# Products with the values in an attention kernel: summing their two parts before the transposes instead of after

## The chip, the cores and the metric

One core of one Trainium2 chip. The metric is the device time of one execution in microseconds; the table below gives the median of three runs.

## The reference

One layer over 2048 tokens of width 1024, in float32: `h = RMSNorm(x) @ w_in`, four groups of four attention heads of width 64 on the columns of `h`, and an output projection with a residual. Cut to what the change touches:

```python
# A: dilated attention, (window, rate) in (128,1), (512,4), (2048,16), merged by softmax denominators
# B: sliding window of 128 with sinks      C: differential attention, two softmax maps
# D: compressed / selected / sliding-window branches, gated
p = exp(scores + bias - max)            # 128 queries by their keys, per head
o = (p @ v) / den                       # every group and branch ends in such a product
y = concat(o_A, o_B, o_C, o_D) * silu(gate)
x = x + y @ w_out
```

## The kernel before

All matrix products run in a float32 form whose operands are split into a high and a low part (`xh`/`xl`, `ph`/`pl`), because one pass over the high part alone would lose digits. The values lie in SBUF as tiles of 128 keys by 128 columns: 64 columns high part, 64 columns low part. A product with the values (`prods`, L407 to L423) uses such a tile as the stationary operand and moves the transposed probabilities past it, once `ph`, once `pl`. So one PSUM tile `o` of 128 partitions collects, for up to four tiles of 128 queries side by side, the transposed output twice: partitions 0 to 63 hold the products with the high part of the values, partitions 64 to 127 those with the low part. Their sum is the output.

A *unit* is such a tile's worth of work: two query tiles of one head in groups C (32 units) and in the selected branch of D (32), four query tiles or heads in the sliding-window branch of D (16), its compressed branch (16), group A (48, the last 16 of them for rate 1, "A1") and group B (16): 160 units, 64 of two tiles and 96 of four. There is one PSUM bank for `o` (pool `ps_o`, bufs=1), so the first product of the next unit waits until the bank is free. At the end of a unit, inside `drive` (L368 to L373), ScalarE copies the bank to the SBUF tile `ot`, and that copy alone frees the bank. Later the unit's `close` calls `o_turn` (L429 to L449): TensorE transposes `ot` in blocks of 128 columns (L434), and the two halves of each transposed block are added on the way out of PSUM, either by one VectorE reduction (L438) or by a ScalarE copy (L441) and a VectorE addition (L443). Where the unit has row weights (`wt`: one over the denominator, times a gate), GpSimd multiplies by them afterwards (L447).

The order of the work is made when the program is written out: `drive` keeps a planned time per engine (`T`), a planned time at which each PSUM bank comes free (`take`, `give`) and a list of steps that wait for a planned time (`defer`). It issues whichever step is planned ready first: transposing a finished unit's `ot`, products, transposing probabilities (`turn_bank`, L392 to L402), scores. When none is ready it issues *filler*: projections of later groups (L832), and later the output projection (L2147). The output projection runs over the token tiles twice, first with the groups C and D (384 matmuls, available when the selected branch has stored a tile), then with A and B (available when A1 and B have stored one). Every engine then runs its instructions in the written order.

On DMA queues nothing is issued by the lines that change.

Of the kernel before, what the change touches and what calls it, by code (L numbers as in the profile page):

```python
# [102 lines left out]
def tile_hybrid_heads(ctx, tc, a):  # L103
# [34 lines left out]
    TILT = -100.0  # L138
# [80 lines left out]
    def give(slot, t):  # L219
        ring[slot[0]][slot[1]] = t  # L220
# [93 lines left out]
    def drive(units, nbuf=3, depth=2, eager=lambda left: False):  # L314

        us, steps = [], []
        tq, pq, cq = [], [], []
        tdone = []

# [7 lines left out]

        while len(us) < len(units) or steps or tq or pq or cq:
            poll()
# [33 lines left out]
            elif c[1] == 1:  # L363
# [3 lines left out]
                if bi == len(u["banks"]) - 1:  # L367
                    u.get("after", lambda: None)()  # L368
                    ot = u["pool"].tile([128, u["n"] * 128], F32, name="ot", bufs=1)
                    A.activation(ot, u["po"][:, :u["n"] * 128], AF.Copy)  # L370
                    e = op("ACT", av(u["n"] * 128), T["PE"] + 120.0)
                    give(u["slot"], e)
                    cq.append((k, e, ot))  # L373
            elif c[1] == 2:
# [6 lines left out]
            elif c[1] == 3:  # L381
                steps.pop(0)[1]()
            else:
                fill_step()

    def turn_bank(u, bi):
# [42 lines left out]
    def o_turn(ot, n, dst, wt=None):  # L429

        slot = take("pt")
        ps = ps_t.tile([128, 512], F32, name="pt")
        for i in range(n):
            PE.transpose(ps[:, i * 128:(i + 1) * 128], ot[:, i * 128:(i + 1) * 128], ident)  # L434
        e = op("PE", 109.0 * n) + 60.0
        p3 = ps[:, :n * 128].rearrange("p (t c) -> p t c", c=128)
        if max(T["DVE"], max(T["ACT"], e) + av(n * 64) + 120.0) + vv(n * 64) > max(T["DVE"], e) + vv(n * 128) + TILT:
            V.tensor_reduce(dst, p3.rearrange("p t (i d) -> p t d i", i=2), AX.X, OP.add)  # L438
            e = op("DVE", vv(n * 128), e)
        else:  # L440
            A.activation(dst, p3[:, :, 0:64], AF.Copy)  # L441
            e = op("ACT", av(n * 64), e)
            V.tensor_tensor(dst, dst, p3[:, :, 64:128], op=OP.add)  # L443
            e = op("DVE", vv(n * 64), e)
        give(slot, e)
        if wt is not None:
            G.tensor_tensor(dst, dst, wt.unsqueeze(2).broadcast_to([128, n, 64]), op=OP.mult)  # L447
            e = op("POOL", 147.0 + 1.67 * n * 64, e)
        return e  # L449
# [1776 lines left out]
```

## Time and profile before

| | |
|---|---|
| median of three runs (lowest, highest) | 1803.11 us (1802.24, 1807.85) |
| the profiled execution: its time, its span | 1810.59 us, 1808.8 us |
| busy: TensorE (PE), VectorE (DVE), ScalarE (ACT), GpSimd (POOL) | 95%, 74%, 59%, 38% of the span |
| chain that ended last | PE 72%, DVE 11%, DMA 6% |

PE rows are matmuls and transposes, PEld rows weight loads beside them. A matmul's row lasts longer than the time to the next one's start, since they are pipelined; the price of one in a series is the distance between starts. `x4` in a time line means four in a row; the number in brackets is idle time of the engine and what ended it.

### The profile page before, as it was taken

How to read it: one execution, taken by the hardware profiler on the slowest of the kernel's cores; microseconds unless marked ns; L12 is line 12 of the kernel's file. 1: busy time of each engine (PE TensorE's matmuls, PEld its weight loads, DVE VectorE, ACT ScalarE, POOL GpSimd, SP SyncE). 2: the span in 40 equal slices, each digit the busy share in tenths (PEclk: the TensorE clock that was granted, in tenths of full speed). 3: DMA queues.
4: the chain of work that ended last, by engine and by line, in shares of the span. 5: the costliest groups of instructions: out<-in, count | busy, mean ns of one | idle time of the engine just before them, and what ended most of it. 6: DMA issues, size and time to landing. Idle time of an engine off the chain costs nothing.

```text
span 1808.8 us, 31757 instructions
## 1 busy us (share of the span) xinstructions
PE 1720.8 (95%) x10035; PEld 1515.1 (84%) x10035; DVE 1335.6 (74%) x4072; ACT 1067.6 (59%) x2582; POOL 695.0 (38%) x841
## 2 busy tenths in 40 slices
PE   7999999899989999799999999999989999989998
PEld 6878878788778888688888789999979999779876
DVE  5446788888898888388855858888576777878873
ACT  4445556665575665366745647676566666567661
POOL 4667653545454455311245552322311111422331
PEclk9999999999999999899999999999999999999999
DMA  7763655235353533653276542332276878889975
GB/s 241 227 205 115 184 161 173 80 105 178 104 164 91 188 98 116 188 153 90 68 215 201 160 134 58 109 100 81 83 232 196 245 241 277 244 267 280 327 247 187
DMA packets 283480, 308.24 MB, mean 170 GB/s; under 512 B 80256, under 2 KB 201216, under 8 KB 282640
## 3 DMA queue, kind: packets, MB, share of 16 engines
q1 hardware_dynamic: 283312, 306.21, 55.1%
q8 instruction: 80, 1.31, 0.3%
q14 instruction: 88, 0.72, 0.1%
HBM read 219.47 MB, written 86.92 MB: 169 GB/s over the span
## 4 chain that ended last, share of the span: by engine, by line
PE 72%; DVE 11%; DMA 6%; issue 3%; ACT 2%; SPq 2%; POOL 2%; DVEq 0%; ACTq 0%; POOLq 0%
PE j L832 27%; PE o L421 11%; PE pt L392 9%; PE j L2147 9%; PE s L942 6%; PE s L1638 4%; PE pt L434 3%; SPq L156 2%; PE s L1328 2%; DVE pl L402 2%; DVE wb L621 1%; DMA wb<-tkA 1%; DVE pa L944 1%; PE pt L740 1%; DMA tc<-sq 1%
## 5 line engine op out<-in xcount | busy, mean ns | idle before, releaser
L832 PE MATMUL j<-wb,xh 128*128 128x512 f32 (+2 forms) x2048 | 622.9, 385 | 20.1 <-ACT wb L617 8.4
L832 PEld LDWEIGHTS j<-wb,xh 128*128 128x128 f32 x2048 | 374.3, 192 | 69.3 <-DVE wb L621 13.0
L832 PE MATMUL j<-wb,xl 128*128 128x512 f32 (+2 forms) x1024 | 386.8, 378 | 0.6 <-POOL xl L576 0.6
L398 ACT ACTIVATE ph<-pt 128x512 fp32r<-128x512 f32 (+4 forms) x486 | 264.2, 575 | 155.0 <-PE pt L392 140.6
L402 DVE TENSOR_TENSOR pl<-pt,ph 128x512 fp32r<-128x512 f32 (+4 forms) x486 | 311.6, 659 | 38.9 <-ACT ph L398 37.8
L832 PEld LDWEIGHTS j<-wb,xl 128*128 128x128 f32 x1024 | 195.3, 191 | 26.3 <-POOL xl L576 1.5
L678 POOL TENSOR_TENSOR ss<-ss,expo 128x6 f32<-128x6 f32 (+2 forms) x64 | 116.2, 1816 | 227.2 <-DVE ss L676 172.6
L576 POOL TENSOR_TENSOR xl<-xt,xh 128x512 fp32r<-128x512 f32 x112 | 151.8, 1355 | 9.3
L370 ACT ACTIVATE ot<-o 128x512 f32<-128x512 f32 (+1 forms) x160 | 81.4, 509 | 109.4 <-PE o L421 108.6
L2101 POOL TENSOR_TENSOR xt<-xt,sq 128x512 f32<-128x512 f32 x32 | 41.1, 1286 | 232.1 <-DVE sq L2099 167.6
L942 PE MATMUL s<-keys,Q 128*128 128x512 f32 (+3 forms) x320 | 112.7, 397 | 7.9 <-DVE mx L944 4.6
L570 POOL TENSOR_SCALAR xh<-xt 128x512 fp32r<-128x512 f32 x128 | 83.3, 651 | 91.8 <-DMA xt<-in_xt_dram 49.4
L944 DVE CUSTOM_DVE_ANT_0 prow<-s,Hs 128x512 f32<-128x512 f32 (+3 forms) x160 | 94.7, 606 | 19.2 <-PE s L942 18.4
L944 DVE CUSTOM_DVE_ANT_0 pa<-s,H 128x512 f32<-128x512 f32 (+3 forms) x160 | 93.8, 604 | 17.1 <-PE s L942 16.6
L1058 DVE SCALAR_TENSOR_TENSOR pa<-pb,ra,pa 128x1024 f32<-128x1024 f32 (+4 forms) x96 | 101.9, 1089 | 2.3
L944 DVE CUSTOM_DVE_ANT_0 pb<-s,H 128x512 f32<-128x512 f32 (+3 forms) x160 | 93.3, 604 | 9.9 <-PE s L942 9.7
L1654 ACT ACTIVATE ap<-ap,AO 128x128 f32<-128x128 f32 (+1 forms) x192 | 86.4, 456 | 13.4 <-DVE AO L1648 13.1
L673 DVE TENSOR_REDUCE ss<-sq 128x6 f32<-128x384 f32 (+2 forms) x64 | 39.4, 615 | 72.2 <-ACT sq L663 71.4
L659 ACT ACTIVATE stqk<-j 128x512 f32<-128x512 f32 x64 | 38.2, 597 | 90.5 <-PE j L832 90.5
L434 PE MATMUL pt<-ident,ot 128*128 128x128 f32 x512 | 85.2, 279 | 5.5 <-DVE pl L402 3.2
L1042 ACT ACTIVATE pa<-pa,nm 128x128 f32<-128x128 f32 (+7 forms) x64 | 76.9, 1202 | 18.7 <-DVE nm L950 18.5
L1042 ACT ACTIVATE pb<-pb,nm 128x128 f32<-128x128 f32 (+7 forms) x64 | 76.8, 1201 | 14.2 <-DVE nm L950 14.1
(266 smaller groups left out, 4222.6 us busy)
## 6 DMA issues: line engine op xcount, KB each, us to landing
xt<-in_xt_dram SPq DMA_DIRECT2D x128, 256.0 KB, 3.5
xr<-in_x_dram SPq DMA_DIRECT2D x16, 512.0 KB, 5.6
Q<-tqC SPq DMA_DIRECT2D x64, 128.0 KB, 3.4
DQ<-tqD SPq DMA_DIRECT2D x16, 512.0 KB, 4.9
raw<-gate_d SPq DMA_DIRECT2D x32, 256.0 KB, 4.7
stqk<-in_x_dram SPq DMA_DIRECT2D x32, 256.0 KB, 4.6
acc_d<-stqk SPq DMA_DIRECT2D x32, 256.0 KB, 3.6
stqk<-acc_d SPq DMA_DIRECT2D x32, 256.0 KB, 4.3
```

Source lines behind the costliest of these rows:

```text
L392: PE.transpose(ps[:rows, x * 128:(x + 1) * 128], src(), ident)
L398: A.activation(ph[:rows, :n], ps[:rows, :n], AF.Copy)
L402: V.tensor_tensor(pl[:rows, :n], ps[:rows, :n], ph[:rows, :n], op=OP.subtract)
L421: PE.matmul(u["po"][:, c0:c0 + wd], lhsT=lhsT(), rhs=x[:rows, col:col + wd], start=u["k"] == 1, stop=u["k"] == total, skip_group_check=True)
L434: PE.transpose(ps[:, i * 128:(i + 1) * 128], ot[:, i * 128:(i + 1) * 128], ident)
L576: G.tensor_tensor(l, xt, h, op=OP.subtract)
L678: G.tensor_tensor(ss[:, :nh], ss[:, :nh], expo[:, :nh], op=OP.pow)
L832: PE.matmul(ps[:, :n], lhsT=xx[:, ks], rhs=W[k][ww][:, lo:hi], start=(k == 0 and i == 0), stop=(k == KT - 1 and i == 2))
L942: PE.matmul(ps[:, :n], lhsT=q(), rhs=k[:, k0:k0 + n], start=(i == 0), stop=(i == np_ - 1))
L944: V.tensor_tensor_reduce(st["row"][:, k0:k0 + n], ps[:, :n], rev(H, t * 128 + 127 - k0, n), 1.0, LOW, OP.add, OP.max, st["mx"][:, ci:ci + 1])
L1042: A.activation(row[:, :nk], row[:, :nk], AF.Exp, bias=nm, accum_out=den[:, i, m:m + 1])
L2147: PE.matmul(ps, lhsT=xx[:, ks], rhs=OW[half, (k, c)][ww], start=(x == 0 and k == 0 and i == 0), stop=(x == len(halves) - 1 and k == 3 and ...
```

## The change

`o_turn` no longer adds halves. Right behind a unit's last product, `half_sums` forms the sum in the transposed layout: ScalarE copies the low part of the first half of the columns to partitions 0 to 63 of `ot` and the high part of the second half to partitions 64 to 127; VectorE adds the other part from PSUM onto each. `ot` is now half as wide, with the first half of the query tiles in the upper 64 partitions and the second half in the lower, and has two buffers instead of one. The bank `o` is free after the second addition. `o_turn` transposes half as many blocks and reads them once, on VectorE together with the row weights, or on ScalarE with the GpSimd multiplication behind it; a planned comparison picks. The planner counts the new steps.

```diff
-                    ot = u["pool"].tile([128, u["n"] * 128], F32, name="ot", bufs=1)
-                    A.activation(ot, u["po"][:, :u["n"] * 128], AF.Copy)
-                    e = op("ACT", av(u["n"] * 128), T["PE"] + 120.0)
-                    give(u["slot"], e)
-                    cq.append((k, e, ot))
+                    summing.append(k)
+                    half_sums(u, lambda ot, e, k=k: turned(k, ot, e))
...
+    def half_sums(u, then):
+        po, m = u["po"], u["n"] * 64
+        ot = u["pool"].tile([128, m], F32, name="ot", bufs=2)
+        A.activation(ot[0:64], po[64:128, 0:m], AF.Copy)
+        e1 = op("ACT", av(m), T["PE"] + 120.0)
+        A.activation(ot[64:128], po[0:64, m:2 * m], AF.Copy)
+        e2 = op("ACT", av(m), T["PE"] + 120.0)
+
+        def add():
+            V.tensor_tensor(ot[0:64], po[0:64, 0:m], ot[0:64], op=OP.add)
+            op("DVE", vv(m), e1)
+            V.tensor_tensor(ot[64:128], po[64:128, m:2 * m], ot[64:128], op=OP.add)
+            e = op("DVE", vv(m), e2)
+            give(u["slot"], e)
+            then(ot, e)
+        defer(e1, add)
...
-        for i in range(n):
+        k = n // 2
+        for i in range(k):
             PE.transpose(ps[:, i * 128:(i + 1) * 128], ot[:, i * 128:(i + 1) * 128], ident)
...
-            V.tensor_reduce(dst, p3.rearrange("p t (i d) -> p t d i", i=2), AX.X, OP.add)
-            e = op("DVE", vv(n * 128), e)
+        on_dve = max(T["DVE"], e) + vv(n * 64) < max(T["ACT"], e) + av(n * 64) + (0.0 if wt is None else 600.0)
+        if on_dve:
+            if wt is None:
+                V.tensor_copy(dst, src)
+            else:
+                V.tensor_tensor(dst, src, w4, op=OP.mult)
...
+            A.activation(dst, src, AF.Copy)
             e = op("ACT", av(n * 64), e)
-            V.tensor_tensor(dst, dst, p3[:, :, 64:128], op=OP.add)
...
+            if wt is not None:
+                G.tensor_tensor(dst, dst, w4, op=OP.mult)
```

Over the whole program the written order has 512 transposes of `ot` before and 256 now; on ScalarE 160 copies out of `o` before and 320 of half the width now; on VectorE no addition onto `ot` before and 320 now. Which operation empties the transposed block changes too: 86 VectorE reductions and 74 ScalarE copies, each with a VectorE addition, before; 63 VectorE multiplications, 6 VectorE copies and 91 ScalarE copies now. The GpSimd multiplications by row weights go from 112 to 49.

Three places of the written order, before and with the change (line numbers of the change are its own: L434 became L455, L421 L441, L392 L412, L832 L859, L942 L969, L2147 L2174).

ScalarE at a unit's end late in the program, before:

```order
L1957 ACTIVATE ap,bden<-ap,bnm 128x256 x2
L370 ACTIVATE ot<-o 128x512
L398 ACTIVATE ph<-pt 128x512
L1957 ACTIVATE ap,bden<-ap,bnm 128x256 x2
L441 ACTIVATE AO<-pt 128x4x64
```

and with the change:

```order
L2142 ACTIVATE xh<-pt 128x512
L392 ACTIVATE ot<-o 64x256
L394 ACTIVATE ot<-o 64x256
L418 ACTIVATE ph<-pt 128x512
L1681 ACTIVATE ap,AO<-ap,AO 128x256 x4
L470 ACTIVATE AO<-pt 128x4x64
```

One copy became two of half the width, and the first VectorE addition waits for a count that only the second copy raises.

TensorE around the last projection matmul (`j<-wb`), in the selected branch of group D (`Qs`, `Qb` are its queries, `prow` probabilities, `VSs` values), before:

```order
L832 MATMUL j<-wb,xh 128x416 x2
L832 MATMUL j<-wb,xl 128x416
L740 MATMUL pt<-ident,stqk 128x128 x8
L942 MATMUL s<-keys,Qs 128x512
L942 MATMUL s<-keys,Qb 128x512
```

and with the change:

```order
L859 MATMUL j<-wb,xh 128x416 x2
L859 MATMUL j<-wb,xl 128x416
L441 MATMUL o<-ph,VSs 128x256
L441 MATMUL o<-pl,VSs 128x256
L441 MATMUL o<-ph,VSs 128x256
L441 MATMUL o<-pl,VSs 128x256
L412 MATMUL pt<-ident,prow_13249 128x128
```

The last projection moved forward. From it to the next filler, the first output matmul, 119 matmuls stand before and 338 with the change (132 products with `VSs`, 121 transposes of probabilities, 66 score matmuls in 33 chunks, 19 other transposes). By the first score of this branch 2730 projection matmuls have been written before, 2832 now.

TensorE behind the last output matmul of groups C and D, in the stage of A1 (`s<-wb` scores, `o<-..,wb` products) and B (`BK,BQ` scores, `BV` products), before:

```order
L2147 MATMUL j<-wb,xl 128x512
L1638 MATMUL s<-wb 128x256 x4
L392 MATMUL pt<-ident,ap 128x128 x4
L1638 MATMUL s<-wb 128x256 x4
L421 MATMUL o<-ph,wb 128x256
```

and a piece of the same stage with the change:

```order
L441 MATMUL o<-ph,BV 128x256
L441 MATMUL o<-pl,BV 128x256
L455 MATMUL pt<-ident,ot 128x128 x2
L1665 MATMUL s<-wb 128x128 x2
L1665 MATMUL s<-wb 128x256 x6
L1967 MATMUL s<-BK,BQ 128x256 x8
L412 MATMUL pt<-ident,ap 128x128 x7
```

Here 112 matmuls stand between the last output matmul of C and D and the first of A and B before, and 254 with the change (78 products, 80 score matmuls, 70 transposes of probabilities, 18 of `ot`, 8 others), and a unit's `ot` is transposed right behind its last product. By the first score of B, 219 output matmuls have been written before, 330 now.

## Rows read from the trace of the kernel before

**Rows 1.** The page: busy time of each engine, instructions.

```profile
PE 1720.8 (95%) x10035; PEld 1515.1 (84%) x10035; DVE 1335.6 (74%) x4072; ACT 1067.6 (59%) x2582; POOL 695.0 (38%) x841
```

**Rows 2.** The page: the chain that ended last, by engine.

```profile
PE 72%; DVE 11%; DMA 6%; issue 3%; ACT 2%; SPq 2%; POOL 2%; DVEq 0%; ACTq 0%; POOLq 0%
```

**Rows 3.** Time line of PE: start, length, engine, line, count; series of transposes and their successors.

```profile
1289.67 0.38 PE L434 MATMUL pt<-ident,ot 128*128 128x128 f32 x2
1289.81 0.36 PE L421 MATMUL o<-ph,VSs 128*128 128x256 f32 x1
...
1315.93 0.60 PE L740 MATMUL pt<-ident,stqk 128*128 128x128 f32 x4
1316.29 0.48 PE L942 MATMUL s<-keys,Qs 128*128 128x512 f32 x1
```

**Rows 4.** Groups by form: busy us, mean ns | idle before.

```profile
L370 ACT ACTIVATE ot<-o 128x512 f32<-128x512 f32 x96 | 57.0, 594 | 68.8 <-PE o L421 68.1 <-ACT xh L2115 0.2
L370 ACT ACTIVATE ot<-o 128x256 f32<-128x256 f32 x64 | 24.4, 381 | 40.6 <-PE o L421 40.5
...
L441 ACT ACTIVATE O<-pt 128x128 f32<-128x128 f32 x14 | 3.9, 278 | 7.4 <-PE pt L434 5.0 <-DMA yC<-O 2.4
...
L402 DVE TENSOR_TENSOR pl<-pt,ph 64x512 fp32r<-64x512 f32 x4 | 2.6, 670 | 0.0
...
L438 DVE TENSOR_REDUCE AO<-pt 128x256 f32<-128x512 f32 x30 | 20.7, 690 | 19.3 <-PE pt L434 19.0
L438 DVE TENSOR_REDUCE Os<-pt 128x128 f32<-128x256 f32 x21 | 8.9, 425 | 13.5 <-PE pt L434 12.9 <-POOL Os L1545 0.6
...
L443 DVE TENSOR_TENSOR AO<-AO,pt 128x256 f32<-128x256 f32 x18 | 7.5, 415 | 1.8 <-ACT AO L441 1.7
...
L443 DVE TENSOR_TENSOR O<-O,pt 128x128 f32<-128x128 f32 x14 | 3.8, 268 | 2.1 <-ACT O L441 2.1
```

**Rows 5.** Time line of all engines: from a unit's last product to its transposes.

```profile
1611.02 0.28 PE L421 MATMUL o<-pl,wb 128*128 128x128 f32 x1
...
1611.33 0.60 ACT L370 ACTIVATE ot<-o 128x512 f32<-128x512 f32 x1
...
1611.98 0.66 PE L434 MATMUL pt<-ident,ot 128*128 128x128 f32 x4 [0.23 <-ACT ot L370]
```

**Rows 6.** Windows: length, busy us (instructions) by engine, granted clock; A, then the stretches without filler.

```profile
1365.00:1527.00 162.00, 161.80 (x984) 151.99 (x983) 114.74 (x435) 104.10 (x356) 27.84 (x19) 1.00 0.79 246
...
1310.50:1339.90 29.40, 24.75 (x122) 17.65 (x120) 23.80 (x65) 19.68 (x32) 2.66 (x3) 0.88 0.81 271
1606.00:1630.60 24.60, 18.40 (x114) 16.17 (x113) 16.73 (x62) 14.62 (x45) 8.59 (x14) 0.79 0.76 226
```

**Rows 7.** Time line: VectorE in the second stretch.

```profile
1607.04 0.41 DVE L1643 CUSTOM_DVE_ANT_0 ap<-s,wb 128x256 f32<-128x256 f32 x1
...
1607.38 0.42 DVE L1643 CUSTOM_DVE_ANT_0 ap<-s,wb 128x256 f32<-128x256 f32 x1
...
1617.60 1.28 DVE L402 TENSOR_TENSOR pl<-pt,ph 128x512 fp32r<-128x512 f32 x2
```

**Rows 8.** Time line of PE: products at full and at the lower clock.

```profile
1290.01 0.28 PE L421 MATMUL o<-pl,VSs 128*128 128x256 f32 x1
1290.13 0.28 PE L421 MATMUL o<-ph,VSs 128*128 128x256 f32 x1
...
1620.80 0.42 PE L421 MATMUL o<-ph,BV 128*128 128x256 f32 x1
1621.01 0.41 PE L421 MATMUL o<-pl,BV 128*128 128x256 f32 x1
```

**Rows 9.** Waits of PE: us in total, times, longest.

```profile
PE o L421 <- DVE pl L402: 13.4, 17, 2.3
...
PE s L942 <- DVE mx L944: 8.0, 13, 2.6
...
PE pt L434 <- ACT ot L370: 1.5, 4, 0.6
```

More of the change, by code (lines that the diff above doesn't have):

```diff
@@ L317, in drive @@
         tq, pq, cq = [], [], []
-        tdone = []
+        tdone, summing = [], []
         def new_unit():
@@ L326, in new_unit, with turned @@
                 tq.append((len(us) - 1, bi))
-        while len(us) < len(units) or steps or tq or pq or cq:
+        def turned(k, ot, e):
+            summing.remove(k)
+            cq.append((k, e, ot))
+        while len(us) < len(units) or steps or tq or pq or cq or summing:
             poll()
@@ L432, in o_turn @@
         ps = ps_t.tile([128, 512], F32, name="pt")
-        for i in range(n):
+        k = n // 2
+        for i in range(k):
             PE.transpose(ps[:, i * 128:(i + 1) * 128], ot[:, i * 128:(i + 1) * 128], ident)
-        e = op("PE", 109.0 * n) + 60.0
-        p3 = ps[:, :n * 128].rearrange("p (t c) -> p t c", c=128)
-        if max(T["DVE"], max(T["ACT"], e) + av(n * 64) + 120.0) + vv(n * 64) > max(T["DVE"], e) + vv(n * 128) + TILT:
-            V.tensor_reduce(dst, p3.rearrange("p t (i d) -> p t d i", i=2), AX.X, OP.add)
-            e = op("DVE", vv(n * 128), e)
+        e = op("PE", 109.0 * k) + 60.0
+        src = ps[:, :n * 64].rearrange("p (i h d) -> p h i d", h=2, d=64)
+        dst = dst.rearrange("p (h i) d -> p h i d", h=2)
+        if wt is not None:
+            w4 = wt.rearrange("p (h i) -> p h i", h=2).unsqueeze(3).broadcast_to([128, 2, k, 64])
+        on_dve = max(T["DVE"], e) + vv(n * 64) < max(T["ACT"], e) + av(n * 64) + (0.0 if wt is None else 600.0)
[4 more added lines that the diff above has]
+                V.tensor_tensor(dst, src, w4, op=OP.mult)
+            e = op("DVE", vv(n * 64), e)
+            give(slot, e)
         else:
-            A.activation(dst, p3[:, :, 0:64], AF.Copy)
+            A.activation(dst, src, AF.Copy)
             e = op("ACT", av(n * 64), e)
-            V.tensor_tensor(dst, dst, p3[:, :, 64:128], op=OP.add)
[L444 to L448, printed above, removed]
+            give(slot, e)
+            if wt is not None:
+                G.tensor_tensor(dst, dst, w4, op=OP.mult)
+                e = op("POOL", 147.0 + 1.67 * n * 64, e)
         return e
```

## The prediction

> **What bounds the kernel now.** I read the page first: TensorE is busy for 95% of the span, VectorE 74%, ScalarE 59% [rows 1]. The chain of waits that ended last says the same: 72% of it is TensorE, 11% VectorE, 6% transfers [rows 2]. So an instruction taken off TensorE is worth about its step, wherever TensorE has something else ready. The windows show where it has: in group A's first stage TensorE is busy for 161.8 of 162 us and VectorE for 114.7 [rows 6]. They also show two stretches where it has not: from the last projection to the first output matmul (1310.5 to 1339.9) and from the last output matmul of C and D to the first of A and B (1606.0 to 1630.6). There the planner has no filler, VectorE is busy for 23.8 of 29.4 and 16.7 of 24.6 us, and the granted clock averages 0.88 and 0.79. A product that follows the next after 0.12 us elsewhere takes 0.21 us there, the 1.2 instead of the 2.4 GHz level [rows 8]. What happens to these stretches decides how much of a TensorE saving is kept.
>
> **The sum goes against the profiled execution** (1810.59 us; 7.5 us, 0.4%, above the median 1803.11). The difference found is then taken off the median. Repeated measurements of this kernel cannot tell less than about 0.3%, 5.4 us, from no change.
>
> **Transposes removed, 256.** A series of two has its successor 0.14 us after its start, one of four 0.36 us [rows 3]: two more cost 0.22, so 0.11 us each. 256 x 0.11 = **28.2 us less** on TensorE. For the same transposes the Trainium skill, "TensorE: Matmul & The Clock Gate", section "Wait — 56ns, not 53.3ns?", gives 55.6 ns from start to start for 128 columns at full clock. By it the removal would be worth 256 x 0.0556 = 14.2 us. The rows of these float32 transposes say twice that, and I take the rows.
>
> **ScalarE.** 96 copies of 594 ns and 64 of 381 ns go (81.4 us) [rows 4]. 320 half-wide ones come: 192 of 256 columns at the 381 ns of that width, 128 of 128 columns at the 278 ns of that width, 109 us. The transposed block leaves through ScalarE 91 times instead of 74, some 5 us. In all +33 us on an engine busy for 59% of the span: hidden, except for the order in which it delivers (below).
>
> **VectorE.** 320 additions come. Half the partitions cost the same as all: a subtraction over 64 partitions took 670 ns, as long as over 128 (1.28 us for two in a row, 0.64 each) [rows 4, 7]. So 192 x 0.415 + 128 x 0.268 = 114 us. 86 reductions go (47 of 0.69, 39 of 0.42: 49 us) and 74 additions (49 of 0.415, 25 of 0.27: 27 us). 69 multiplications or copies come (39 of 0.415, 30 of 0.27: 24 us). Net **+62 us**, 74% of the span becoming some 78%. GpSimd, busy for 38%, loses 63 multiplications.
>
> Where TensorE is full this is covered, but not all of it. TensorE waited 13.4 us for the low halves of the transposed probabilities and 8.0 us for score maxima, both from VectorE [rows 9]. VectorE's busy time grows by 5%; if such waits grow by no more, that is 1 us, if VectorE's lag doubles them in its fullest stages, 10 us. I take **+4 us**, nearer the low end since the planner counts the new passes and writes the followers later.
>
> **The bank `o` and the transposes come later.** Before, the copy starts 0.31 us after the last product's start and lasts 0.60, and the transposes follow 0.96 us after that start [rows 5]. Now the first addition waits for both copies: 0.31 + 0.28 + 0.38, then two additions of 0.41, about 1.8 us. So **0.8 us more per unit**, both for the transposes and for the next unit's first product, which needs the only bank. Counting what the written order puts behind a unit's last product (0.11 us a transpose, 0.12 us per 256 columns), 21 of 160 units now have less than the wait needs (3 before), short by 12 us in all, 10 of it in 13 units of A1 and B. Most of these lie in the second stretch and are counted there; for the others **+2.5 us**.
>
> **The filler moves forward.** To bridge the longer wait the planner spends filler sooner: 102 more projection matmuls before the selected branch, 111 more output matmuls before group B. These are no extra work, but the two stretches without filler grow.
>
> First stretch: from 119 matmuls to 338. TensorE's own steps: 140 transposes at 0.11, 132 products at 0.12, 66 score matmuls of 13 us: 44 us (18 us before). VectorE: 33 score chunks at 0.64 for 512 columns and 0.34 for 256, 18 us; 30 subtractions at 0.64, 19; 14 half additions, 4; closes and the gates of two output tiles, 7: 48 us. The stretch before is mostly scores, each waiting for a bank that VectorE empties; the new one is mixed, and both engines are nearly level. At least it takes 48 us, at VectorE's share of before (23.8 of 29.4) 59. TensorE then loses 4 to 15 us against 11 before: -7 to +4, taken as **+1 us**.
>
> Second stretch: from 112 matmuls to 254, whose own steps are 28.5 us (12.7 before). VectorE's 16.7 us per 112 matmuls [rows 6] make 38 us, with half additions in place of the old ones 42. The pace of before, 24.6 us per 112, would make 56. That pace contains a wait for a load that a longer stretch need not repeat, but the new one has nine closes with 0.8 us more each, several with transposes right behind the last product. I take 48. TensorE loses 19.5 us there against 11.9: **+7.6 us** (bounds +2 and +16).
>
> **Sum:** -28.2 + 4 + 2.5 + 1 + 7.6 = **-13 us**, so 1797.5 us on the profiled execution's scale and **1790 us** against the median, 0.7% less. Chance 0.43.
>
> **Rivals.**
>
> *The whole saving arrives.* The stretches are VectorE's in both kernels, and the loads that held up the second one get time. Then only 2 us are lost: 1777 us. For it: the first stretch is level on both engines. Against: the half additions land exactly where VectorE leads. Chance 0.18.
>
> *The stretches eat it.* The second runs at the pace of before (+16), the first gains 4, VectorE's lag costs 8: 28 us, no change, 1803 us. For it: the clock fell in both stretches before, and fewer TensorE steps beside VectorE's keep it low longer. Chance 0.21.
>
> *Slower: TensorE waits for the bank.* One bank, and now two engines in turn must empty it. The first product of the next unit stands in TensorE's order at a planned time; behind it stand filler and scores that could run. If VectorE reaches the additions late, everything behind stands. The order covers 139 units, so the lag of VectorE decides: from 13 / 139 = 0.09 us per unit nothing is left of the gain, from 0.13 us it is slower by over 0.3%. A single subtraction of 0.64 us ahead of every third addition is 0.2 us, 28 us, hence 1818 us. For it: VectorE already makes products wait in 17 places, up to 2.3 us [rows 9]. Against: the copy that freed the bank until now made the transposes wait 1.5 us in all. Chance 0.16.
>
> *The transposes are cheap.* If a transpose is worth its 0.05 us between others, the removal brings 14 us and the losses above take them: 1802 us, no change. This is where the rule of the page named above leads; the trace speaks against it, with 0.22 us for two. Chance 0.02.
>
> That the change does not do what it says has no room: the written order has 256 transposes instead of 512.
>
> **Numbers.** Faster by over 0.3% (under 1797.7): 0.43 + 0.18 = 0.61. Within: 0.21 + 0.02 = 0.23. Slower: 0.16. The range runs from 1773 us (the whole saving, with a stretch shortened) to 1811 us, which takes in the no-change cases and half of the slower one.
>
> **What would show it.** 256 transposes of `ot`, TensorE's busy time down by nearly the removed steps; VectorE up by some 60 us, ScalarE by some 30. The window without filler in D near 50 us, that of A1 and B near 48, both with the clock below full in places. Among TensorE's waits, new ones for `ot` from VectorE of a few us in all. The forecast is wrong if those waits come to over 10 us outside the stretches, if the second stretch lasts over 55 us, or if neither stretch lengthens.

## The result: 0.6% slower, and the profile after

The changed kernel takes 1814.55 us (median of 4 runs, 1813.19 to 1816.95), the kernel before 1804.71 us (4 runs, 1802.24 to 1807.85). The ratio is 1.0061, with a 95% interval of 1.0038 to 1.0083. I had forecast 1790 us and a gain; the time lies outside the range that I gave, on the other side. The profiled execution of the changed kernel took 1816.95 us, its span is 1815.2 us.

The first view is the page's table of busy time, to be read against [rows 1].

```profile
PE 1706.4 (94%) x9779; PEld 1489.1 (82%) x9779; DVE 1409.2 (78%) x4301; ACT 1120.2 (62%) x2759; POOL 661.6 (36%) x778
```

The 256 transposes are gone from TensorE, and its busy time fell by 14.4 us, half of the 28.2 that I had taken for them. VectorE's rose by 73.6 us (I had 62), ScalarE's by 52.6 (I had 33).

The groups by line show the new close. Its columns are busy time, mean ns of one, then the idle time of the engine ahead of them and what ended it. L392 and L394 are ScalarE's two half copies, L398 and L400 VectorE's two half sums, L455 the transposes.

```profile
L455 PE MATMUL pt<-ident,ot 128*128 128x128 f32 x256 | 58.6, 291 | 30.6 <-DVE ot L400 26.7 <-DVE pl L422 3.3
L400 DVE TENSOR_TENSOR ot<-o,ot 64x256 f32<-64x256 f32 (+1 forms) x160 | 59.9, 374 | 2.2
L398 DVE TENSOR_TENSOR ot<-o,ot 64x256 f32<-64x256 f32 (+1 forms) x160 | 57.2, 358 | 54.1 <-ACT ot L394 50.8 <-PE j L859 1.7 <-PE pt L412 1.2
L392 ACT ACTIVATE ot<-o 64x256 f32<-64x256 f32 (+1 forms) x160 | 54.2, 339 | 78.7 <-PE o L441 76.6
L394 ACT ACTIVATE ot<-o 64x256 f32<-64x256 f32 (+1 forms) x160 | 53.4, 334 | 1.9
```

The sums cost VectorE 117.1 us (I had 114), and VectorE stood another 54.1 us ahead of them, nearly all of it waiting for ScalarE's copies. TensorE's waits answer to [rows 9]; the line of the low halves is now L441 <- L422, that of the score maxima L969 <- L971.

```profile
PE pt L455 <- DVE ot L400: 26.7, 31, 2.9
PE o L441 <- DVE pl L422: 10.0, 14, 1.4
PE s L969 <- DVE mx L971: 8.3, 10, 2.6
...
PE o L441 <- DVE ot L400: 0.9, 1, 0.9
```

The transposes waited 1.5 us for ScalarE's copy before [rows 9]; now they wait 26.7 us for VectorE's sums: 13.7 us in the second stretch without filling work, 0.8 in the first, 12.1 outside both. The two waits for VectorE that the kernel before had, for low halves and score maxima, did not grow (13.4 to 10.0 and 8.0 to 8.3 us). The bank `o` itself, which the slower rival was about, was waited for once, 0.9 us. One such close, in the second stretch without filling work, on the time line of all engines:

```profile
1567.52 0.28 PE L441 MATMUL o<-pl,BV 128*128 128x256 f32 x1
...
1567.84 0.38 ACT L392 ACTIVATE ot<-o 64x256 f32<-64x256 f32 x1 [0.46 <-PE o L441]
...
1568.23 0.38 ACT L394 ACTIVATE ot<-o 64x256 f32<-64x256 f32 x1
...
1568.95 0.41 DVE L398 TENSOR_TENSOR ot<-o,ot 64x256 f32<-64x256 f32 x1
...
1569.37 0.43 DVE L400 TENSOR_TENSOR ot<-o,ot 64x256 f32<-64x256 f32 x1
...
1569.86 0.69 PE L455 MATMUL pt<-ident,ot 128*128 128x128 f32 x2 [2.06 <-DVE ot L400]
```

From the last product's start to the first transpose it is 2.34 us, against 0.96 in [rows 5]; 0.34 us of that VectorE was still at other work when the second copy was done. The windows without filling work, to be read against the last two of [rows 6] (length, then busy time and instructions by engine, granted clock):

```profile
1247.30:1310.60 63.30, 54.67 (x341) 44.82 (x339) 52.95 (x158) 45.53 (x94) 10.12 (x18) 0.93 0.57 178
1560.90:1626.70 65.80, 43.10 (x257) 37.47 (x255) 51.30 (x200) 40.62 (x127) 14.04 (x24) 0.79 0.81 243
```

The first lasts 63.3 us (my sum, with +1 us over the loss of before, makes it 56; my list of signs says near 50, which does not fit that sum), the second 65.8 (I had 48). By TensorE's own steps as I had worked them out (44 and 28.5 us), 19 and 37 us are lost in them, against 11 and 12 before.

### The profile page after: what moved, and what is told of

It reads as the page before. It is cut to its first block, busy times and chain, and to the rows that moved or that the text cites. A ratio compares the mean times of both kernels' runs of the same rounds, so it can differ in the third digit from the quotient of the medians.

```text
span 1815.2 us, 31735 instructions
## 1 busy us (share of the span) xinstructions
PE 1706.4 (94%) x9779; PEld 1489.1 (82%) x9779; DVE 1409.2 (78%) x4301; ACT 1120.2 (62%) x2759; POOL 661.6 (36%) x778
## 5 line engine op out<-in xcount | busy, mean ns | idle before, releaser
L859 PE MATMUL j<-wb,xh 128*128 128x512 f32 (+2 forms) x2048 | 617.6, 382 | 14.8 <-ACT wb L644 7.4
L859 PEld LDWEIGHTS j<-wb,xh 128*128 128x128 f32 x2048 | 373.1, 190 | 65.0 <-DVE wb L648 11.2
L859 PE MATMUL j<-wb,xl 128*128 128x512 f32 (+2 forms) x1024 | 384.8, 376 | 1.0 <-POOL xl L603 1.0
L422 DVE TENSOR_TENSOR pl<-pt,ph 128x512 fp32r<-128x512 f32 (+4 forms) x486 | 311.5, 659 | 23.1 <-ACT ph L418 21.2
L859 PEld LDWEIGHTS j<-wb,xl 128*128 128x128 f32 x1024 | 194.2, 190 | 26.7 <-POOL xl L603 1.9
L969 PE MATMUL s<-keys,Q 128*128 128x512 f32 (+3 forms) x320 | 113.2, 393 | 10.9 <-DVE mx L971 6.0
L971 DVE CUSTOM_DVE_ANT_0 prow<-s,Hs 128x512 f32<-128x512 f32 (+3 forms) x160 | 94.6, 605 | 19.4 <-PE s L969 18.3
L1085 DVE SCALAR_TENSOR_TENSOR pa<-pb,ra,pa 128x1024 f32<-128x1024 f32 (+4 forms) x96 | 106.1, 1132 | 2.3
L971 DVE CUSTOM_DVE_ANT_0 pa<-s,H 128x512 f32<-128x512 f32 (+3 forms) x160 | 93.9, 604 | 14.1 <-PE s L969 12.3
L392 ACT ACTIVATE ot<-o 64x256 f32<-64x256 f32 (+1 forms) x160 | 54.2, 339 | 78.7 <-PE o L441 76.6
L398 DVE TENSOR_TENSOR ot<-o,ot 64x256 f32<-64x256 f32 (+1 forms) x160 | 57.2, 358 | 54.1 <-ACT ot L394 50.8
L971 DVE CUSTOM_DVE_ANT_0 pb<-s,H 128x512 f32<-128x512 f32 (+3 forms) x160 | 93.5, 604 | 7.3 <-PE s L969 6.4
L455 PE MATMUL pt<-ident,ot 128*128 128x128 f32 x256 | 58.6, 291 | 30.6 <-DVE ot L400 26.7
L1069 ACT ACTIVATE pb<-pb,nm 128x128 f32<-128x128 f32 (+7 forms) x64 | 76.9, 1202 | 11.9 <-DVE nm L977 11.3
```

Of the source, the lines that this page charges most:

```text
L422: V.tensor_tensor(pl[:rows, :n], ps[:rows, :n], ph[:rows, :n], op=OP.subtract)
L859: PE.matmul(ps[:, :n], lhsT=xx[:, ks], rhs=W[k][ww][:, lo:hi], start=(k == 0 and i == 0), stop=(k == KT - 1 and i == 2))
L969: PE.matmul(ps[:, :n], lhsT=q(), rhs=k[:, k0:k0 + n], start=(i == 0), stop=(i == np_ - 1))
L971: V.tensor_tensor_reduce(st["row"][:, k0:k0 + n], ps[:, :n], rev(H, t * 128 + 127 - k0, n), 1.0, LOW, OP.add, OP.max, st["mx"][:, ci:ci + 1])
L1069: A.activation(row[:, :nk], row[:, :nk], AF.Exp, bias=nm, accum_out=den[:, i, m:m + 1])
L1085: V.scalar_tensor_tensor(rows[i][:, k0:k0 + n], part[i][:, k0:k0 + n], ra[:, 1:2], rows[i][:, k0:k0 + n], op0=OP.mult, op1=OP.add)
```

## The experiments

Ratios are to runs of the kernel before in the same set (medians 1804.1 to 1806.0 us), with 95% intervals. Diffs are against the changed kernel unless said otherwise.

### In which stage

**C and D alone, A and B alone.** A unit carries a flag that chooses the old close or the new.

```diff
-                    summing.append(k)
-                    half_sums(u, lambda ot, e, k=k: turned(k, ot, e))
+                    if u["half"]:
+                        summing.append(k)
+                        half_sums(u, lambda ot, e, k=k: turned(k, ot, e))
+                    else:
...
```

> Half sums in C and D (its window, compressed and selected branches) alone; A and B close as before, with a copy of the whole product and four transposes. After stood about 10 us ahead of before when A's scores began (1354.8 against 1365.2) and lost all its ground behind that. Theory 'latency': TensorE waits behind the last product for two copies and two sums where no filling work is left, which is above all in A and B; then this kernel keeps the 10 us: 1795 (1788 to 1800). Rival 'load': VectorE's 70 us more work is what costs, spread over the stages by their share of units (64 of the 160 sums' units stand in A and B): 1808 to 1812. Rival 'first stretch': the loss lies at D's end (63 us without filling work in place of 29): no better than 1804.

> Half sums in A and B alone; C and D close as before. Theory 'latency': the stage that has filling work (C, D) gave the 10 us and A and B lose about 20, so without C and D's gain this is 1820 to 1828, slower than the whole change. Rival 'load': between before and after, 1807 to 1812. Rival 'first stretch': faster than before, 1795 to 1802, since A and B would then only gain.

Measured: C and D alone 1803.04 us, ratio 0.9988 (0.9965 to 1.0011); A and B alone 1818.01 us, 1.0080 (1.0057 to 1.0104). So A and B lose 0.8%, and C and D together do not gain what the trace had suggested: no theory had both right. The 10 us by which the changed kernel seemed ahead at A's first score were not its own. The kernel with A and B alone has the order of the kernel before on TensorE through C and D, and its trace reaches that score at 1355.6 us, the changed kernel's at 1354.8; the profiled execution of the kernel before, at 1365.2, was one of its slower ones (1810.59 us).

**C alone.**

> Half sums in C alone, where filling work lies beside every close (no stretch without it before the end of D); D, A and B close as before. 64 transposes fewer, 7 us by 0.11. The order behind C has the stretches of before (119 and 112 matmuls without filling work at D's end and in B, against 338 and 254 in after). 'Cover' (the close's wait is hidden where filling work is to be had, and the price is the filling work that is missing later): 1799 to 1806 against 1805 to 1806, a gain of no more than 6 us. 'Load' (VectorE's sums cost in C as elsewhere, 0.2 us for each us of sums): the gain is eaten, 1804 to 1810.

Measured: 1792.05 us, 0.9936 (0.9914 to 0.9959): **faster than both kernels**, and by twice the 6 us that I had allowed. Its two stretches without filling work are those of [rows 6] again:

```profile
1290.50:1319.90 29.40, 24.87 (x122) 17.60 (x121) 23.79 (x65) 19.65 (x32) 2.72 (x3) 0.88 0.81 271
1584.00:1608.10 24.10, 16.69 (x115) 14.77 (x115) 16.35 (x62) 14.31 (x44) 8.25 (x13) 0.93 0.77 235
```

Made in C alone the change gains 0.6%; with D it loses most of that (from -0.6% to -0.1%), with A and B more (to +0.6%). But not all of the 12 us is gained in C. From the first score of C to its last product this trace takes 606.1 us, against 615.6 in the kernel before and 610.0 in the kernel with A and B alone, which has the order of before there. D's window and compressed branches close as before, with as much filling work beside them (663 and 660 projection matmuls), and yet take 331.4 us against 341.3 and 337.5. What differs there is the order in which the planner placed that work.

### The saving by itself

**Half of the transposes left out of the kernel before**; the transposed half is read twice, so half of the heads' outputs are not computed.

```diff
-        for i in range(n):
+        for i in range(n // 2):
             PE.transpose(ps[:, i * 128:(i + 1) * 128], ot[:, i * 128:(i + 1) * 128], ident)
```

> The kernel before with every second transpose of the close left out (the rest is read twice, so half of the heads get the wrong values): TensorE loses the same 256 transposes, and nothing else changes but the plan's knowledge of it. All theories: the 28 us of 256 by 0.11 us come through but for what the stretches without filling work give back, 1776 to 1788. If it is above 1795, the transposes taken out were never worth 28 us, and the saving itself was mis-sized.

Measured: 1770.47 us, 0.9789 (0.9757 to 0.9821), 35.5 us less than before. The saving is real, and 7 us more than 256 times 0.11. TensorE's busy time falls by 37.2 us there. Why it is more was not tried. Against it stand losses of 45 us in the change (these 35.5 and the 9.8 by which it is slower), where I had summed 15.

### The plan's part

**The plan books the half sums, and none is made.** In the kernel without half of the transposes, and in the kernel before:

```diff
-                    e = op("ACT", av(u["n"] * 128), T["PE"] + 120.0)
-                    give(u["slot"], e)
-                    cq.append((k, e, ot))
...
+                    e1 = op("ACT", av(m), T["PE"] + 120.0)
+                    e2 = op("ACT", av(m), T["PE"] + 120.0)
...
+                        op("DVE", vv(m), e1)
+                        e = op("DVE", vv(m), e2)
+                        give(u["slot"], e)
...
+                        cq.append((k, e, ot))
+                    defer(e1, booked)
```

> The kernel with half of the transposes left out (1770.5), with its instructions' order planned as if the half sums were there: the plan books the two sums on VectorE, the later end of the close and the later release of the bank, and no sum is made. Theory 'plan' (filling work is handed out earlier to cover a close that the plan takes to be longer, and is missing later): 1782 to 1795. Otherwise 1768 to 1775.

> The kernel before, all four transposes and its single copy, with its order planned as if the half sums were there (as in the kernel above). Theory 'plan': 12 to 20 us slower than before, 1817 to 1826. Otherwise within 4 us of before, 1801 to 1809.

Measured: 1795.13 us, 0.9947 (0.9930 to 0.9965), against 0.9789 without the booking; and 1816.51 us, 1.0065 (1.0041 to 1.0090), on the kernel before. An order made for a longer close costs 0.6 to 1.6% although no close is longer. The windows without filling work, first of the kernel with half of the transposes, then of the same with the sums booked:

```profile
1278.40:1307.20 28.80, 23.55 (x120) 15.93 (x118) 23.97 (x64) 20.17 (x32) 2.84 (x3) 0.94 0.84 274
1552.60:1591.20 38.60, 28.49 (x184) 24.10 (x184) 29.83 (x128) 27.65 (x90) 11.86 (x19) 0.90 0.84 261
```

```profile
1239.80:1288.90 49.10, 40.36 (x261) 34.63 (x260) 37.89 (x114) 33.83 (x73) 8.54 (x15) 0.90 0.77 238
1526.50:1604.70 78.20, 52.22 (x314) 44.72 (x313) 58.74 (x212) 47.17 (x147) 25.92 (x35) 0.81 0.68 207
```

The second stretch grew from 184 to 314 TensorE instructions, and from 38.6 to 78.2 us with the clock from 0.90 to 0.81: the output matmuls that stood in it were spent earlier. The two traces lose nothing up to A's first score (1333.8 us without the booking, 1331.7 with it) and 25 us from there to the last output matmul (430.9 against 455.7).

**One entry of the plan at a time**, in the kernel without half of the transposes, again without any sum: VectorE's time alone, then the later close and release of the bank alone.

```diff
+                    defer(e, lambda u=u, e=e: op("DVE", 2 * vv(u["n"] * 64), e))
```

```diff
-                    give(u["slot"], e)
-                    cq.append((k, e, ot))
...
+                        e3 = e + 2 * vv(u["n"] * 64)
+                        give(u["slot"], e3)
...
+                        cq.append((k, e3, ot))
+                    defer(e, booked)
```

> Half of the transposes left out as in the kernel that ran in 1770.5, and of the half sums only VectorE's time is booked in the plan (close and release of the bank as before, no sum is made). Theory 'booked load' (the plan takes VectorE to be late, so it has TensorE do filling work while it waits in the plan, early, and the stages at the end of D and in A and B have none): close to the plan with everything booked (1795.1), 1788 to 1798. Theory 'booked close' (the later end of the close makes the plan do that): 1768 to 1776.

> The counterpart: half of the transposes left out, the plan books the close and the bank later by the two sums' time, but no work for VectorE. 'Booked close': 1788 to 1798. 'Booked load': 1768 to 1778.

Measured: 1801.14 us, 0.9981 (0.9969 to 0.9993), and 1796.62 us, 0.9956 (0.9941 to 0.9971). Each entry alone costs as much as both, so neither theory is right as I had put it. The second kernel's stretches are short (28.4 and 37.2 us), so what it loses is lost elsewhere: by its trace 4 us in C, 7 in D and 8 from A's first score on. TensorE waits 16.3 us for score maxima in it, against 6.2 in the kernel without the booking. That the order planned for the sums costs 0.6% on the kernel before and some 1.6% without half of the transposes is shown; that all of it is the stretches is not. A rival was not tried: that any small change of the planner's numbers moves the time by such amounts. One entry that costs as much as both, and D's pace in the kernel with C alone, leave room for it.

**The sums are made and the plan does not know.** First nothing is booked (the diff), then VectorE's time alone, by an `op("DVE", 2 * vv(m), e)` behind the sums.

```diff
-        e1 = op("ACT", av(m), T["PE"] + 120.0)
...
-        e2 = op("ACT", av(m), T["PE"] + 120.0)
+        e = op("ACT", av(2 * m), T["PE"] + 120.0)
...
-            op("DVE", vv(m), e1)
...
-            e = op("DVE", vv(m), e2)
...
-        defer(e1, add)
+        defer(e, add)
```

> The whole change, all sums made, the complete result; only the plan knows nothing of the sums: they go into VectorE's order at the planned end of the copies, no time of VectorE is booked for them, and close and bank end in the plan with the copies. Theory 'booked load': the 24.6 us that the plan cost without any sum come back, and what is left is the saving of 35.5 us against VectorE's real lag of 19 to 24: 1787 to 1798, faster than before. Rival 'cover': the filling work that the plan hands out early covers waits for VectorE that are real, and taken away they fall on TensorE: 1808 to 1825.

> As the kernel with nothing booked, but with the sums' time booked on VectorE; close and bank end in the plan with the copies. 'Booked load': no better than 1803, 1803 to 1814. 'Cover' or 'booked close': 1790 to 1800.

Measured: 2074.76 us, 1.1491 (1.1447 to 1.1535), and 2021.84 us, 1.1195 (1.1176 to 1.1214): the clearest misses of the study. The waits of TensorE in the first of them:

```profile
PE pt L452 <- DVE ot L398: 218.6, 142, 4.6
```

In 142 of 160 closes TensorE stood for the sums, 1.5 us each. So the wait is real in nearly every unit, and the plan of the changed kernel hides it: only 31 such waits were left there. "Cover" was the right theory, though its own times (1808 to 1825, and 1790 to 1800 for the second kernel) were far too low. The price is the filling work, which is no extra work but is then missing later.

### VectorE's part

These kernels have the order of the changed kernel on TensorE, instruction by instruction (9,779 in both traces), so that only the sums differ.

**The sums left out** (the low parts are not added).

```diff
-            V.tensor_tensor(ot[0:64], po[0:64, 0:m], ot[0:64], op=OP.add)
...
-            V.tensor_tensor(ot[64:128], po[64:128, m:2 * m], ot[64:128], op=OP.add)
```

> The whole change with VectorE's two sums per unit left out (the low parts are not added; 320 instructions of VectorE fewer, about 110 us less than... no more than 115 us of its time), while the order on every other engine stays that of after, since the plan still books them. TensorE's half transposes then wait for ScalarE's copies alone. Theory 'latency': the 26.7 us of waits of the transposes for the sums fall to about 10 and the clock drops get fewer: 1790 to 1798. Rival 'plan': the filling work was spent too early, the order is the same, so the time stays within 5 us of after, 1810 to 1815. Rival 'load': as 'latency', 1785 to 1798; the next kernel parts these two.

Measured: 1788.12 us, 0.9907 (0.9873 to 0.9940): 26 us less than the change. "Plan" alone is out: the order by itself still leaves a gain of 0.9%. But the two stretches are as long as in the changed kernel, or nearly:

```profile
1231.20:1288.70 57.50, 50.95 (x340) 43.20 (x339) 47.85 (x140) 45.05 (x94) 9.94 (x18) 0.97 0.64 195
1533.80:1598.90 65.10, 43.32 (x257) 38.18 (x255) 44.92 (x183) 40.36 (x127) 14.66 (x24) 0.79 0.82 245
```

So the order makes the stretches long, not the sums. Against the kernel before without half of its transposes, whose trace takes 430.9 us from A's first score to the last output matmul, this one takes 447.7; up to A's first score it is not slower (1331.8 against 1333.8). Where the sums cost, the starts of the same instruction in both traces show (us, and how far the changed kernel is behind):

```
TensorE instruction   without sums   with sums   behind
3600 (C)                   699.9        703.2       3.2
4800 (D, window's end)     917.7        924.8       7.0
5600 (D, selected begins) 1062.4       1076.6      14.2
7200 (D's end)            1307.2       1329.7      22.5
8800 (B)                  1596.1       1623.7      27.6
9600 (B's end)            1733.2       1764.3      31.1
```

That is some 3 us in C, which ends at instruction 3729, 20 in D and 9 from A's first score on. The two traces also show at which instructions, since every distance from one start to the next can be set beside its twin: of the 32 us, 31 are added ahead of the transposes of `ot`. (It is so in sum. In D half of the loss lies there; in A and B up to the first output matmul 13 us are added there and 8 come back at others.) TensorE's idle time ahead of the transposes agrees, 30.6 us with the sums and 7.5 without:

```profile
L453 PE MATMUL pt<-ident,ot 128*128 128x128 f32 x256 | 55.8, 279 | 7.5 <-ACT ot L394 4.4 <-DVE pl L420 2.9
```

So in the changed kernel the price of the sums is paid where TensorE waits for them.

**The sums made, but the transposes do not wait for them.** They are written back into the bank (the low parts do not reach the output); then they add a constant, which was meant to take away their wait for the copies too.

```diff
+            V.tensor_tensor(po[0:64, 0:m], po[0:64, 0:m], ot[0:64], op=OP.add)
...
+            V.tensor_tensor(po[64:128, m:2 * m], po[64:128, m:2 * m], ot[64:128], op=OP.add)
```

> The whole change, but VectorE's sums are written back into the bank of the products and not into the tile that TensorE transposes: VectorE's work and its order stay those of after, the bank is held as long, and only the transposes no longer wait for the sums (the low parts don't reach the output). Theory 'latency': nearly as without the sums, 1792 to 1802. Rival 'load': as after, 1811 to 1816. Rival 'plan': as after, 1810 to 1816.

> As the kernel with the sums put aside, but each sum adds a constant tile to the products in place of ScalarE's copy: VectorE's work and the holding of the bank stay, only the wait of the sums for the copies goes (in after VectorE stood 54.1 us idle ahead of them, 50.8 of it put down to ScalarE). The low parts don't reach the output. Theory 'blocked queue': what hurts is that VectorE, which works in order, stands still for the copies with the low parts and maxima of the next units behind it; then 1796 to 1806 (half of the 34 us between the kernel without sums, 1788.1, and that with the sums aside, 1822.7, or more comes back). Theory 'load': it is the 120 us of sums themselves, 1815 to 1823.

Measured: 1822.67 us, 1.0103 (1.0070 to 1.0136), and 1824.65 us, 1.0093 (1.0065 to 1.0121). Both are as slow as the changed kernel or slower. But the wait did not go, it moved to the bank; in the first of the two kernels:

```profile
PE o L441 <- DVE o L400: 10.7, 16, 2.1
```

Of the 37 and 34 us that the two traces lose against the one without sums, 26 and 23 are added ahead of the products with `ph`, the first of a unit among them. So these runs show that moving the wait gains nothing, not that the wait costs nothing. Nor do they decide on "blocked queue": the sums of the second kernel write the bank that ScalarE's copies read, and VectorE stood for those copies as before, 32.7 us ahead of the larger form and 11.9 ahead of the smaller, against 50.8 in the changed kernel:

```profile
L399 DVE TENSOR_TENSOR o<-o,ident 64x256 f32<-64x256 f32 x96 | 40.8, 425 | 36.8 <-ACT ot L394 32.7 <-PE pt L413 1.8
```

**Load alone**: two additions of constants into a tile that nobody reads, the bank free after the copies. (The tile of the transposes has one buffer here in place of two.)

> As the kernel without the sums, plus two instructions of the sums' size per unit on VectorE that add constants and write a tile which nobody reads: VectorE has the sums' load in the sums' place, but they wait for nothing, the bank of the products is free after ScalarE's copies, and the half transposes wait for the copies alone. Theory 'load': most of the 34 us between the kernel without sums (1788.1) and those with sums that nobody reads (1822.7, 1824.7) is there, 1810 to 1823. Theory 'hold' (the one bank of the products is kept until VectorE, late in its own order, has read it, and the next unit's products stand behind it): 1786 to 1797.

Measured: 1812.11 us, 1.0041 (1.0020 to 1.0062): 24 us more than without sums, with nothing waiting for them and VectorE not standing ahead of them. So VectorE's time costs by itself, with a caveat: these additions took more time than the sums, 142.4 us in place of 117.1. By that share the time of the sums would be worth 20 of the 26 us, an estimate. Here the loss is spread over projections, scores and products, 3 of 33 us at the transposes; in the changed kernel it shows at the transposes. Which of the two, VectorE's time or its place in the close, is the cause there stays open: in every one of these kernels that kept VectorE's work the time was lost, at one place or another.

```profile
L403 DVE TENSOR_TENSOR junk<-ident 64x256 f32<-64x256 f32 (+1 forms) x160 | 73.7, 461 | 2.2
L401 DVE TENSOR_TENSOR junk<-ident 64x256 f32<-64x256 f32 (+1 forms) x160 | 68.7, 429 | 0.0
```

### Other places for the sum

**Later in VectorE's order**, at `defer(e2 + 250.0, add)` in place of `defer(e1, add)`.

> The whole change, with the two sums put into VectorE's order later, 0.25 us behind the planned end of the second copy in place of the planned end of the first, and the plan told so. 'Blocked queue': VectorE has other work to do until the copies are there, so it waits less and the time falls, 1800 to 1809. 'Load': VectorE's work is the same and each close ends 0.6 us later in the plan, so 1813 to 1822.

Measured: 1819.82 us, 1.0071 (1.0052 to 1.0091), as the change: no gain, although VectorE stood 37 us ahead of the sums in place of 54.

**On GpSimd, and from one copy.** First ScalarE copies four quarters and GpSimd adds 128 rows at once; then ScalarE copies the bank in one piece and VectorE adds its lower and upper rows.

```diff
+        A.activation(oy[0:64], po[0:64, 0:m], AF.Copy)
+        A.activation(oy[64:128], po[64:128, m:2 * m], AF.Copy)
...
+            G.tensor_tensor(ot, oy, ot, op=OP.add)
```

```diff
+        A.activation(x, po[:, 0:2 * m], AF.Copy)
...
+            V.tensor_tensor(x[0:64, 0:m], x[0:64, 0:m], x[64:128, 0:m], op=OP.add)
+            V.tensor_tensor(x[64:128, 0:m], x[0:64, m:2 * m], x[64:128, m:2 * m], op=OP.add)
```

> The sums move from VectorE to GpSimd: ScalarE copies all four quarters (two copies per unit more, 320 in all by 0.34 us, some 54 us on an engine that is busy for 62%), GpSimd adds the 128-row tiles in one instruction, and the bank is free after the copies. The close gets longer by about 1 us. 'Load' and 'blocked queue': VectorE is rid of 117 us of sums and 54 us of standing still, so 1792 to 1803, faster than before. 'Latency' (the waiting of the half transposes behind a longer close): slower than after, 1816 to 1830.

> The whole result is computed, by another way: ScalarE copies the whole bank to SBUF in one instruction as the kernel before does, which frees the bank there, and VectorE then makes the two half sums between the lower and the upper rows of that copy. Half transposes as in after. 'Hold': 1795 to 1804, at or below before. 'Load': VectorE's sums stay, so 1808 to 1816.

Measured: 1836.70 us, 1.0156 (1.0118 to 1.0194), and 1845.52 us, 1.0225 (1.0197 to 1.0253). Both are worse than the change, but neither is a clean test. The first adds 99 us of work to ScalarE (I had counted 54), and TensorE now waits 17.8 us for the bank and 17.2 for GpSimd's sums. In the second the sums take 146.8 us of VectorE in place of 117.1, and the transposes wait for them as long as in the change (29.1 us); that the bank comes free early could bring little, since it was hardly waited for. In both the tile of the transposes has one buffer in place of two.

**On TensorE**, in the kernel before: a product with two unit matrices above each other turns and sums at once.

```diff
-            PE.transpose(ps[:, i * 128:(i + 1) * 128], ot[:, i * 128:(i + 1) * 128], ident)
+            PE.matmul(ps[:, i * 64:(i + 1) * 64], lhsT=ot[:, i * 128:(i + 1) * 128], rhs=ident2[0], start=True, stop=True)
```

> Another way to the same complete result, built on the kernel before: in the window and compressed branches of D and in A and B, TensorE multiplies each 128 columns of the copied products by two unit matrices above each other (64 columns), so that it turns and sums both parts at once; no sum in front of the transposes, no second sum behind them, the close's length and the plan's booking of TensorE stay those of before, and the eviction reads half as much. (A constant is narrowed from 32 to 16 columns to make room.) C and the selected branch of D close as before. If the lesson is 'the sum may not stand between the products and the transposes': TensorE's time is as before, VectorE loses 0.27 us per close or a whole second addition on 96 of 160 closes, about 30 us of its time, which by the 24 us for 117 us that the kernel with load alone showed is worth some 6 us: 1792 to 1804. If such a product takes TensorE longer than the transpose (its duration is in no row yet), 1805 to 1830.

Measured: 1835.95 us, 1.0186 (1.0162 to 1.0211). TensorE's time line has eight instructions for the four products of a close:

```profile
891.67 1.08 PE L462 MATMUL pt<-ident,ot 128*128 128x64 f32 x8
892.56 0.48 PE L421 MATMUL o<-ph,VW 128*128 128x512 f32 x1
```

The successor starts 0.89 us later, 0.22 us per product, where a transpose is 0.11 [rows 3]. For 96 closes of four that is 384 x 0.11 = 42 us more TensorE work; 32 us were measured.

## Why the prediction was wrong

Taken one behind the other, the runs split the +0.6%, in per cent of the kernel before: half of the transposes away -2.1; the order planned for the sums +1.6; two half copies and the cheaper tail in place of one copy and the old tail, with the order that they bring, -0.4 (within the intervals); the sums themselves +1.5. (The steps are differences between neighbours, so they add up by themselves.)

- **The saving, -28.2 us.** Right in kind, and too small: -35.5 us. The rival of cheap transposes is out. The Trainium skill, "TensorE: Matmul & The Clock Gate", section "Wait — 56ns, not 53.3ns?", has 55.6 ns for a matmul of 128 columns, and with it 14 us, an estimate; no run here bears that out for these float32 transposes.
- **"These are no extra work" and the stretches, +1 and +7.6 us.** The step that failed first. I saw the filling work move forward, gave the longer stretches +8.6 us together and let them go with a bound of +16 for the second. Against their own steps they lose 8 and 25 us more than before. The runs show that the order alone costs 1.6%, 25 us on the median, before a sum is made (0.6% on the kernel before). With everything booked the traces lose it from A's first score on; by the second kernel with one entry booked, not all of it in the stretches.
- **The longer close, +0.8 us per unit, short by 12 us in all, +2.5 us outside the stretches.** The second failed step. In the close shown it is 2.34 us from last product to transposes against 1.8 forecast, and VectorE comes to the sums late. TensorE waited for them in 31 closes, not 21, for 26.7 us, 12.1 of them outside the stretches. At the same order the sums cost 26 us. That so few units are exposed is the plan's work: 1.5 us in each of 142 closes is what it covers.
- **VectorE in the covered stages, +4 us, bounds 1 and 10.** The two waits that I scaled fell by 3 us together. VectorE's additional work did not show there but at the transposes; that it costs elsewhere when nothing waits for the sums, the run with the load alone shows. I had not counted the 54 us that VectorE stands still ahead of the sums; what they cost, no run shows by itself.
- **The slower rival** gave 1818 us, near the time, but by the wrong mechanism, so by luck: TensorE waited for the bank once. The waits came for `ot`, as the last part of the prediction had said, and at 12.1 us outside the stretches they were just over its mark of 10.
- **The mark for a wrong forecast** that I had set, a second stretch over 55 us, was met at 65.8.

With the measured sizes in the terms of my sum, -35.5 - 3.1 + 12.1 + 7.9 + 25.4 us, it comes to some +7 us, an estimate; the profiled executions differ by 6.4.

Open: why half of the transposes bring 35.5 and not 28 us, and C alone 12 us for 64 of them, half of it in D; how much of the order's 1.6% is the longer close and how much any other order; and whether the sums cost by VectorE's time or by their place in the close.

## What to carry to other kernels

A step set between the products of a tile and the next instruction on the bounding engine costs twice: the work that covers its wait is missing where the work runs out, and where the wait is not covered the bounding engine stands for it, or, if the wait is taken away there, for something else of the engine that does the step. Both can be measured before the step is built: leave the removed work out (the ceiling), then let the planner book the new step without making it (the cost of the cover). Between two kernels with the same order, starts set side by side show where the time goes. And such a change need not be made everywhere: in C alone it gained 0.6%, in all stages it lost as much. That C gains because filling work lies beside every close is not shown, since D's window and compressed branches have such work too.

## What was not expected of the hardware

A float32 product of 64 columns was two TensorE instructions of 0.11 us each, the transpose of 128 columns one of 0.11: narrowing the product did not make it cheaper than the transpose.

VectorE's additions of constants over 64 rows were dearer than the sums over 64 rows. The groups by form, first of the changed kernel, then of the one that adds constants:

```profile
L400 DVE TENSOR_TENSOR ot<-o,ot 64x256 f32<-64x256 f32 x96 | 41.0, 427 | 1.3
```

```profile
L403 DVE TENSOR_TENSOR junk<-ident 64x256 f32<-64x256 f32 x96 | 51.6, 538 | 1.3
L1198 DVE TENSOR_TENSOR part<-part 128x256 f32<-128x256 f32 x2 | 0.9, 426 | 0.1
```

It is 427 against 538 ns for the same 256 elements. Both inputs of the dearer one lie in SBUF, where the sum has one in PSUM, but that alone is not the reason: the last line is a product of two SBUF tiles in the same kernel, and it took 426 ns. What made the constants dear was not tried. The Trainium skill, "VectorE: DVE Perf Modes", section "The TRN2 errata", gives (N + 151) / 0.96 ns for a float32 addition, by which 256 elements are 424 ns, an estimate; the sum and the product agree, the additions of constants do not.
